# Reordering both ends of the up stage of a hybrid diffusion layer, and loading the gate rows by DMA

## The chip, the cores and the metric

One core of a Trainium2 chip runs the whole kernel. The metric is the device time of one execution in microseconds (us). The kernel before took 1548.68 us, the median of 3 runs (1547.78 to 1554.11).

The core has a matrix engine (TensorE: PE, with its weight loads listed as PEld), three engines that work on rows of 128 partitions (VectorE: DVE; ScalarE: ACT; GpSimd: POOL), and a queue that only issues transfers (SyncE: SP). Each engine takes its own instructions strictly in order; semaphores tie them together. Work is held in SBUF (on-chip memory, 128 partitions) and in eight PSUM banks of 128 x 512 fp32, into which PE accumulates.

## The reference

One layer with 1152 tokens (1024 latent tokens on a 16 x 64 grid, 128 prompt tokens) of width 1024. The part that this change touches is the second half, the convolutional feed-forward network and its gate:

```python
def conv_ffn(h, w_up, conv_w, conv_b, w_down, grid):
    u = dw_conv(h @ w_up, conv_w, conv_b, grid)
    gate, up = jnp.split(u, 2, axis=-1)
    return (jax.nn.silu(gate) * up) @ w_down
...
    x = x + gate1 * mix
    h = rmsnorm(x, norm2) * (1 + scale2) + shift2
    x = x + gate2 * conv_ffn(h, w_ffn_up, ffn_conv, b_ffn_conv, w_ffn_down, grid)
```

`w_up` is 1024 x 5632, `w_down` 2816 x 1024. `dw_conv` is a depthwise convolution: 3 x 3 over the grid for latent tokens, width 3 for prompt tokens. `gate2` is one row of 1024 numbers for the latent tokens and another for the prompt tokens; both come out of a small matrix product early in the kernel. A final `rmsnorm` gives the outputs.

## The kernel before

**Precision.** Each fp32 operand of a large product is split into a high and a low part; a product is three matmuls: high by high, high by low, low by high. The high part is a copy on ACT, the low part a subtraction on DVE or POOL (`split_lo`, L69).

**Up stage (L1742 and around).** The hidden width is cut into 22 columns of 128 gate channels and the 128 up channels that belong to them. For each column the 2 x 2 block product (two halves of the latent tokens, gate and up channels, with the inner dimension of 1024 in two halves) is done with seven products instead of eight, of twelve matmuls of 128 x 512 each. `up(c, p)` issues product p of column c. In the trace they are told apart by the name of their token operand:

- 1: weights 11 by tokens b11, into X; 2: 12 by b21, into Z; 3: s4 by b22, onto Y; 4: 22 by t4, onto X; 5: s1 by t1, into Y; 6: s2 by t2, onto X; 7: s3 by t3, onto X.
- s1 to s4 and t1 to t4 are sums of weight and of token blocks. ACT copies Y after product 5 (`p5`), X after product 1 (`p1`, named cp in the trace) and X after product 6 (`u2`, named u2p). DVE then adds: F (gate channels, two banks) is Z + p1 and Y + u2; S (up channels, two banks) gets its second half as X (after product 7) + p5 (L2081), and X goes on with product 4. So product 4 can't start before that addition has read X, and product 6 and 7 can't start before their copies.
- `up_prompt(c, half)` issues twelve matmuls of 128 x 256 for the prompt tokens (into a bank of the pool x); `prompt_columns(c)` turns them with two transposes (L1987), and ACT and four short DVE instructions convolve them (L1919, L1923).
- The order on PE from column 2 on: 5, then transposes and 4 of the column before, 2, 3, 1, half the prompt, 6, the other half, 7.
- `conv_rows` convolves F and later S: one ACT instruction with the centre weight (L1894), then eight DVE taps (L1906). Then ACT applies silu (L2000), POOL multiplies (L2002) and stores the result to DRAM (`scr_g`, L2003); every second column POOL also makes and stores sums of tokens (`token_sums`, L1859 to L1863).

F and S tiles take turns in three PSUM buffers of two banks (0 and 1, 2 and 3, 4 and 5): S of column c is written where F of column c - 1 was, F of column c + 1 where S of column c - 1 was. The pool x has banks 6 and 7.

**First column.** Column 0 runs beside the end of the stage before it. Its instructions are chained by hand: `run(eng, fn)` puts each one behind the last of its engine. `first_sums` (L1816) makes on DVE the last token sums, the splits of t4 (high parts `half_hi` on ACT, low parts `half_lo` on DVE, in two pieces of 256 tokens), the split of column 1's s1, the weight sums s2 and s4 of column 1, and F's additions; the addition of S follows behind it. Then `second_pair` splits the other weights of column 1 in pairs, copies on ACT and subtractions on POOL.

**Order elsewhere.** Outside those chains a planner orders each engine's instructions when the kernel is built, from program order and from times that it simulates; `tc.issue_after(x)` pins an instruction behind x on its engine. All products of the up stage are chained on PE (`chained`). The order on each engine's queue is then fixed.

**Down stage (L2199).** The down product is again seven products, each over eleven pairs of weight rows and into four PSUM banks (xb or yb), twelve matmuls to a pair. xb are banks 2, 3, 6, 7; yb are banks 0, 1, 4, 5. Weights and activations of a pair come by DMA into one of six raw buffers and are split into one of seven pairs of buffers (`next_w`, `load_w`: load L129, ACT copy L132, subtraction L69 on POOL for the first six pairs, on DVE after that). The planner is free to order the pairs and banks. The first product uses xb, the second yb. `load_gates` at pair 6 of the first product loads a 128 x 512 tile `modrC` with the rows of both gates from DRAM; `make_gates` at pair 10 has PE spread each gate row over 128 partitions, by four fp32 products of a column of the identity with that tile (L2130), into the yb banks; ACT copies them to SBUF (L2131). `add_gated` uses them when the second product is finished.

## Time and profile before

The profiled execution took 1549.85 us; the span from its first to its last instruction is 1548.1 us.

| what | value |
|---|---|
| median of 3 runs | 1548.68 us |
| profiled execution, its span | 1549.85 us, 1548.1 us |
| PE, DVE, ACT, POOL busy | 1487.8, 1145.5, 783.2, 708.9 us |
| first product of column 0 to first down product | 781.25 to 1290.62 us |
| PE waiting in columns 0 and 1: longest | 5.05 us, until 811.01 |
| PE waiting at the last column's product 4 | 1.57 us, until 1287.74 |
| PE waiting in the first down product | 1.92 us, until 1293.37 |
| gate products on PE | 3.67 us, from 1321.94 |
| PE waiting for the gate copies | 1.63 us, until 1329.97 |
| PE waiting after that | none shown |

How to read the rows that follow. A timeline row has the start in us from the span's start, the length in us, engine, line, operation, output and inputs by the program's names, shapes, count, and in brackets the idle time of that engine ahead of it with what ended it. Consecutive like instructions are merged. Matmuls are pipelined: a row's length overlaps the next one's start, so the step from start to start is what counts. A row of a stretch has its bounds and length, then for each engine the busy time and count of instructions, then the PE clock that was granted (1.00 is full), the share of the DMA engines that were busy, and GB/s. A row of waits has who waited, for whom, the total in us, how many times, and the longest.

### The profile page before, as it was taken

To read this page: it belongs to the slowest core of one execution; us is meant where nothing else is said; L and a number is where in the kernel's file an instruction comes from. 1 tells how busy PE (TensorE), PEld (TensorE's weight loads), DVE (VectorE), ACT (ScalarE), POOL (GpSimd) and SP (SyncE) were. 2 spreads that over 40 slices of the span, in tenths; PEclk is the share of its full clock that TensorE was granted. 3 is DMA by queue.
4 is the path that set the end of the run, shared out by engine and by line. 5 is a ranking of instruction groups with operands and counts; after the bars stand their busy time and mean duration, and the time that the engine had idled before them with its cause. 6 is when DMAs were issued, how large, how long until landed. Compare 5 with 4: busy or idle time off the path is not lost.

```text
span 1548.1 us, 31132 instructions
## 1 busy us (share of the span) xinstructions
PE 1487.8 (96%) x12506; PEld 1255.0 (81%) x12506; DVE 1145.5 (74%) x1731; ACT 783.2 (51%) x1523; POOL 708.9 (46%) x538
## 2 busy tenths in 40 slices
PE   7999999999999989899989999999999999999997
PEld 2699998999898978777767888888888887788886
DVE  3657466664556757655789999999999999579575
ACT  3566567555454544512664444444444444467444
POOL 1412122334233240222227999999999996000001
PEclk9999999999999999999999999999999999999999
DMA  9311121335435362677652555545644666879752
GB/s 339 113 54 47 35 65 51 120 92 189 135 123 182 111 198 80 235 272 278 200 180 77 179 166 128 136 118 146 193 117 135 179 162 200 330 244 360 245 192 115
DMA packets 172940, 252.49 MB, mean 163 GB/s; under 512 B 11733, under 2 KB 113603, under 8 KB 170875
## 3 DMA queue, kind: packets, MB, share of 16 engines
q1 hardware_dynamic: 149591, 172.21, 34.8%
q0 software_dynamic: 22592, 77.60, 16.2%
q8 instruction: 98, 1.61, 0.4%
q10 hardware_dynamic: 611, 0.68, 0.1%
q14 instruction: 48, 0.39, 0.1%
HBM read 190.62 MB, written 82.90 MB: 177 GB/s over the span
## 4 chain that ended last, share of the span: by engine, by line
PE 78%; DMA 6%; DVE 6%; issue 4%; ACT 3%; POOL 2%; SPq 1%; POOLq 0%; ACTq 0%; DVEq 0%
PE u L1742 26%; PE mm L603 13%; PE xb L2199 6%; PE yb L2199 6%; PE mm L617 5%; PE x L1970 4%; PE mm L746 3%; PE lv L935 3%; PE yb L2250 2%; PE u L1512 2%; DVE acc L1906 2%; PE x L1003 1%; PE mm L506 1%; DMA mh<-scr_m 1%; DMA wa<-in_w_ada_dram 1%
## 5 line engine op out<-in xcount | busy, mean ns | idle before, releaser
L1906 DVE SCALAR_TENSOR_TENSOR acc<-u,convc,acc 128x945 f32<-128x945 f32 (+2 forms) x352 | 426.8, 1218 | 7.8 <-ACT acc L1894 0.7
L69 POOL TENSOR_TENSOR wl<-raw,wh 128x1024 fp32r<-128x1024 f32 x42 | 103.6, 2468 | 241.0 <-ACT wh L132 183.2
L603 PE MATMUL mm<-h1h,wh 128*128 128x384 f32 x528 | 186.0, 352 | 0.8 <-ACT qj L515 0.8
L603 PE MATMUL mm<-h1l,wh 128*128 128x384 f32 x528 | 180.0, 341 | 0.0
L603 PE MATMUL mm<-h1h,wl 128*128 128x384 f32 x528 | 180.0, 341 | 0.0
L898 DVE TENSOR_TENSOR Q<-Q,fb 128x384 f32<-128x384 f32 x126 | 86.3, 685 | 90.5 <-PE lv L935 89.0
L69 POOL TENSOR_TENSOR wul<-sr,wuh 128x512 fp32r<-128x512 f32 (+1 forms) x64 | 116.2, 1816 | 19.5 <-ACT wuh L1727 19.3
L69 POOL TENSOR_TENSOR wul<-ra,wuh 128x1024 fp32r<-128x1024 f32 x44 | 112.3, 2552 | 20.3 <-ACT wuh L1727 17.8
L888 ACT ACTIVATE m<-k 128x384 f32<-128x384 f32 x126 | 70.2, 557 | 86.9 <-PE lv L935 39.8
L2174 POOL TENSOR_TENSOR sq<-sq,mhalf 128x1 f32<-128x1 f32 x9 | 11.1, 1231 | 213.3 <-DVE sq L2171 213.3
L603 PEld LDWEIGHTS mm<-h1h,wh 128*128 128x128 f32 x528 | 100.3, 190 | 5.7 <-issue 3.9
L603 PEld LDWEIGHTS mm<-h1l,wh 128*128 128x128 f32 x528 | 100.3, 190 | 0.6 <-issue 0.2
L603 PEld LDWEIGHTS mm<-h1h,wl 128*128 128x128 f32 x528 | 100.0, 189 | 0.8 <-issue 0.5
L617 PE MATMUL mm<-wh,h1h 128*128 128x256 f32 x288 | 83.9, 291 | 0.8 <-ACT v L642 0.8
L900 DVE TENSOR_TENSOR k<-k,fb 128x384 f32<-128x384 f32 x126 | 74.2, 589 | 12.2 <-ACT m L888 6.7
L617 PE MATMUL mm<-wh,h1l 128*128 128x256 f32 x288 | 80.5, 280 | 0.0
L617 PE MATMUL mm<-wl,h1h 128*128 128x256 f32 x288 | 80.4, 279 | 0.0
L132 ACT ACTIVATE wh<-raw 128x1024 fp32r<-128x1024 f32 x50 | 53.0, 1059 | 44.0 <-PE mm L603 11.3
L2002 POOL TENSOR_TENSOR acc<-acc,acc 128x1152 f32<-128x1152 f32 x22 | 60.0, 2729 | 9.8 <-DVE acc L1906 9.8
L1727 ACT ACTIVATE wuh<-ra 128x1024 fp32r<-128x1024 f32 x42 | 44.3, 1055 | 39.5 <-issue 16.6
L1934 ACT ACTIVATE u2p<-u 128x512 f32<-128x512 f32 x44 | 26.4, 601 | 70.1 <-PE u L1742 70.1
L1727 ACT ACTIVATE wuh<-sr 128x512 fp32r<-128x512 f32 (+1 forms) x62 | 48.1, 775 | 24.1 <-PE x L1970 16.1
(387 smaller groups left out, 4485.5 us busy)
## 6 DMA issues: line engine op xcount, KB each, us to landing
ra<-in_w_ffn_up_dram SPq DMA_DIRECT2D x84, 256.0 KB, 3.0
raw<-in_w_in_dram SPq DMA_DIRECT2D x32, 512.0 KB, 4.7
v<-in_w_ada_dram SPq DMA_DIRECT2D x27, 512.0 KB, 4.3
scr_g<-acc POOLq DMA_DIRECT2D x22, 576.0 KB, 5.4
scr_s<-late POOLq DMA_DIRECT2D x11, 1024.0 KB, 5.9
scr_t<-in_w_ffn_down_dram POOLq DMA_DIRECT2D x16, 704.0 KB, 7.2
wa<-in_w_ada_dram SPq DMA_DIRECT2D x16, 512.0 KB, 6.2
scr_t<-in_w_ffn_down_dram POOLq DMA_DIRECT2D x2, 2816.0 KB, 13.5
```

Source lines behind the costliest of these rows:

```text
L69: return eng.tensor_tensor(out, full, hi.bitcast(F32), op=ALU.subtract)
L603: anchor["fill"] = mm(ps, a[:, kt, :], h[kt][b], start=(n == 0), stop=(n == 23))
L617: anchor["fill"] = mm(ps, h[kt][t // 3][:, ts_], a[:, kt % 4, :], start=(n == 0), stop=(n == 23))
L888: nc.scalar.activation(aps(t, 0, [[2 * h, NB], [h, 2], [1, h]]), aps(src, 0, [[2 * h, NB], [BL + h, 2], [1, h]]), AF.Copy)
L898: nc.vector.tensor_tensor(qm, qm, aps(ff_, 2 * h - 1, [[BL - h, 2], [2 * h, NB], [0, h]]), op=ALU.mult)
L900: nc.vector.tensor_tensor(km, km, aps(ff_, BL + 2 * h - 1, [[-(BL + h), 2], [2 * h, NB], [0, h]]), op=ALU.mult)
L1727: first = nc.scalar.activation(hi, raw, AF.Copy)
L1742: last = mm(dst, w_slot(c, a, x)[:, kt, :], HB[y][b][:, kt, :], start=(start and n == 0), stop=(stop and n == 11), skip_group_check=True,)
L1906: last = nc.vector.scalar_tensor_tensor(o, u3[:, r0 + dy : r1 + dy, c0 + dx : c1 + dx], wc(3 * (dy + 1) + dx + 1), o, op0=ALU.mult, op1=AL ...
L1970: last = mm(pk, HB[h]["p"][:, 4 * half + kt, :], aps(flat(W[x]), a * 512 + kt * P, [[(b - a) * 512, 2], [1, P]]), start=(half + kt + n == ...
L2002: last = nc.gpsimd.tensor_tensor(accg, accg, accu, op=ALU.mult)
L2199: anchor["down"] = mm(banks[i], w[a][:, ts_], w[b][:, 512:1024], start=(start and j == 0 and n == 0), stop=(j == NPAIR - 1 and n == 2), sk ...
```

## The change

Four edits, none of which changes what is computed:

1. **First column.** The addition of S and the first addition of F move from the end of DVE's chain to a place right behind the last token sums, ahead of the t4 splits. The low parts of t4 move ahead of the weight sums s2 and s4. The issue of product 7 moves ahead of `first_sums` in the text.
2. **Last column.** Column 21's products go in the order 2, 1, 3, 6, half the prompt, 7, the other half, 4 and then the prompt's transposes, instead of 2, 3, 1, half the prompt, 6, the other half, 7, transposes, 4.
3. **First down banks.** The first three pairs of the first down product are done bank by bank, nine matmuls to a bank, in the order of the banks (2, 3, 6, 7), pinned behind the last product of the up stage.
4. **Gate rows.** The tile `modrC`, the four spreading products and their copies are gone; four DMAs on SP's queue each load a half row of a gate from DRAM into all 128 partitions, at pair 6 of the first down product.

```diff
--- before.py
+++ after.py
@@ -1815,10 +1815,12 @@
 
     def first_sums():
 
-        F = u[0][0]
+        F, S = u[0]
         for n in range(2):
             token_sum(tmp[2 + n], rb(1, 0, n), tmp[2 + n])
         new_tiles("t4", 1)
+        run("dve", lambda: tt(S[:, 512:NS], S[:, 0:512], copies["p5"], op=ALU.add))
+        run("dve", lambda: tt(F[:, 0:512], F[:, 0:512], copies["p1"], op=ALU.add))
         half_hi("t4", 0, tmp[2])
         slot = SLOT[1]["s1"]
         hi, lo = (flat(W[x][:, slot]) for x in "hl")
@@ -1826,11 +1828,10 @@
         run("act", lambda: nc.scalar.activation(hi, raw, AF.Copy))
         run("dve", lambda: split_lo(nc.vector, lo, raw, hi))
         half_hi("t4", 1, tmp[3])
+        for n in range(2):
+            half_lo("t4", n, tmp[2 + n])
         run("dve", lambda: second_sum("s2", "s1", "11", ALU.subtract, nc.vector))
         run("dve", lambda: second_sum("s4", "12", "s2", ALU.subtract, nc.vector))
-        for n in range(2):
-            half_lo("t4", n, tmp[2 + n])
-        run("dve", lambda: tt(F[:, 0:512], F[:, 0:512], copies["p1"], op=ALU.add))
         run("dve", lambda: tt(F[:, 512:NS], F[:, 512:NS], copies["u2"], op=ALU.add))
 
     token_work()
@@ -2022,7 +2023,11 @@
             up(c, 5)
         if c == 0:
             prompt_work()
-        if c > 0:
+        if c == NHID:
+            up(c - 1, 4)
+            prompt_columns(c - 1)
+            second_half(c - 1)
+        elif c > 0:
             prompt_columns(c - 1)
             up(c - 1, 4)
             second_half(c - 1)
@@ -2032,9 +2037,11 @@
             split_slots(n, ("21", "22"), nc.gpsimd)
             if n + 1 < NHID:
                 load_row(n + 1, 2)
+        last_c = c == NHID - 1
         if c > 0:
             up(c, 2)
-            up(c, 3)
+            if not last_c:
+                up(c, 3)
         pks[c] = ps_p.tile([P, 2 * P], F32, name="x", tag="x")
         if c == 1:
             up_prompt(c, 0)
@@ -2042,9 +2049,14 @@
         if c > 0:
             u[c].append(ps_u.tile([P, NS], F32, name="u", tag="u"))
             up(c, 1)
-        if c > 1:
+            if last_c:
+                up(c, 3)
+        if 1 < c and not last_c:
             up_prompt(c, 0)
         up(c, 6)
+        if last_c:
+            up_prompt(c, 0)
+            up(c, 7)
         if c == 0:
             up(c, 3)
             up_prompt(c, 0)
@@ -2055,8 +2067,8 @@
                 load_row(n + 1, 1)
         F, S = u[c]
         if c == 0:
+            up(c, 7)
             first_sums()
-            up(c, 7)
         else:
             nc.vector.tensor_tensor(F[:, 0:512], F[:, 0:512], copies["p1"], op=ALU.add)
             nc.vector.tensor_tensor(F[:, 512:NS], F[:, 512:NS], copies["u2"], op=ALU.add)
@@ -2077,9 +2089,9 @@
         if c > 0 and n:
             split_slots(n, ("s2", "s4"), nc.gpsimd)
         if c > 0:
-            up(c, 7)
-        add_s = lambda: nc.vector.tensor_tensor(S[:, 512:NS], S[:, 0:512], copies["p5"], op=ALU.add)
-        run("dve", add_s) if c == 0 else add_s()
+            if not last_c:
+                up(c, 7)
+            nc.vector.tensor_tensor(S[:, 512:NS], S[:, 0:512], copies["p5"], op=ALU.add)
         anchor["conv"] = conv_rows(F, c, acc[c][0])
         if c == 0:
             ran["act"] = anchor["rows"]
@@ -2113,22 +2125,13 @@
     smp = pool(ctx, "sm2", 1)
     fn = gpp.tile([P, D], F32, name="fn")
     gate2 = {}
-    modr["C"] = gpp.tile([P, 512], F32, name="modrC")
-
     def load_gates():
-        with tc.issue_after(anchor["load"].ins):
-            nc.sync.dma_start(modr["C"], scr_mod["C"])
-
-    def make_gates():
-
         for v in (1, 0):
             gate2[v] = gpp.tile([P, D], F32, name=f"gate2_{v}")
             for half in range(2):
-                pt = ps_c[half].tile([P, 512], F32, name="yb", tag="yb")
                 rr = 32 * (2 + half) + v
-                with tc.issue_after(anchor["down"].ins):
-                    mm(pt, ident[:, rr : rr + 1].to_broadcast([P, P]), modr["C"], start=True, stop=True)
-                nc.scalar.activation(gate2[v][:, HF[half]], pt, AF.Copy)
+                with tc.issue_after(anchor["load"].ins):
+                    nc.sync.dma_start(gate2[v][:, HF[half]], scr_mod["C"][rr : rr + 1, :].to_broadcast([P, 512]))
 
     g_ph = gpp.tile([P, NHID, P], F32R, name="g_ph")
     g_pl = gpp.tile([P, NHID, P], F32R, name="g_pl")
@@ -2185,9 +2188,9 @@
         with tc.issue_after(anchor["load"].ins):
             nc.sync.dma_start(fn, ins["final_norm"].rearrange("(o d) -> o d", o=1).to_broadcast([P, D]))
 
-    def product(banks, start, stop, done, tail=0, beside={}):
-
-        for js in [(j,) for j in range(NPAIR - tail)] + ([tuple(range(NPAIR - tail, NPAIR))] if tail else []):
+    def product(banks, start, stop, done, tail=0, head=0, beside={}):
+
+        for js in ([tuple(range(head))] if head else []) + [(j,) for j in range(head, NPAIR - tail)] + ([tuple(range(NPAIR - tail, NPAIR))] if tail else []):
             ws = [next_w() for _ in js] if len(js) == 1 else next_ws(len(js))
 
             if js[0] in beside:
@@ -2196,14 +2199,15 @@
                 ts_ = slice(i * P, (i + 1) * P)
                 for j, w in zip(js, ws):
                     for n, (a, b) in enumerate(((0, 0), (0, 1), (1, 0))):
-                        anchor["down"] = mm(
-                            banks[i],
-                            w[a][:, ts_],
-                            w[b][:, 512:1024],
-                            start=(start and j == 0 and n == 0),
-                            stop=(j == NPAIR - 1 and n == 2),
-                            skip_group_check=True,
-                        )
+                        with tc.issue_after(anchor["down"].ins) if j < head else nullcontext():
+                            anchor["down"] = mm(
+                                banks[i],
+                                w[a][:, ts_],
+                                w[b][:, 512:1024],
+                                start=(start and j == 0 and n == 0),
+                                stop=(j == NPAIR - 1 and n == 2),
+                                skip_group_check=True,
+                            )
                 if js[-1] == NPAIR - 1:
                     done(i)
 
@@ -2218,8 +2222,9 @@
         return [p.tile([P, 512], F32, name=nm, tag=nm) for p in pool_ for _ in range(2)]
 
     xb = bank(ps_b, "xb")
+    anchor["down"] = ran["pe"]
     p1, u2, u3 = {}, {}, {}
-    product(xb, True, False, copy_bank(p1, "p1"), beside={6: load_gates, 10: make_gates})
+    product(xb, True, False, copy_bank(p1, "p1"), beside={6: load_gates}, head=3)
 
     yb = bank(ps_c, "yb")
 
```

## The prediction

> **What bounds the kernel now.** I read the busy shares first, then stretches of the up stage, then who waits for whom, then the timelines of TensorE (PE), VectorE (DVE), ScalarE (ACT) and GpSimd (POOL) at both ends of the up stage.
>
> ```profile
> PE 1487.8 (96%) x12506; PEld 1255.0 (81%) x12506; DVE 1145.5 (74%) x1731; ACT 783.2 (51%) x1523; POOL 708.9 (46%) x538
> ```
>
> ```profile
> 811.00:816.30 5.30, 5.29 (x13) 4.13 (x14) 4.78 (x7) 2.12 (x4) 4.56 (x4) 0.50 0.19 53
> ...
> 850.00:895.00 45.00, 45.00 (x223) 37.29 (x222) 43.74 (x47) 20.93 (x28) 42.53 (x29) 1.00 0.60 190
> ```
>
> ```profile
> 1294.00:1299.00 5.00, 5.00 (x17) 3.94 (x16) 4.89 (x5) 0.78 (x1) 4.46 (x4) 0.66 1.07 259
> ```
>
> ```profile
> DVE u L2061 <- ACT cp L1934: 1.0, 6, 0.2
> ```
>
> ```profile
> PEld u L1742 <- DVE acc L1906: 6.2, 20, 0.3
> ```
>
> In a stretch row stand the busy times of PE, its weight loads, DVE, ACT and POOL, then the granted PE clock. PE is the bound overall, but in the middle of the up stage (two columns in 45 us) DVE is busy for 43.74 of 45.00 us too. The two hold each other once per column: product 1 (b11) writes the bank that the convolution of the column before has just read (20 waits of 0.3 us on DVE acc L1906), and DVE's first addition waits for the copy of that product (up to 0.2 us). So a gain of PE alone at the front of the up stage is kept only as far as DVE moves too. Two stretches run at half or lowered clock (0.50 and 0.66); each follows an idle PE.
>
> **First column.**
>
> ```profile
> 801.21 0.28 PE L1970 MATMUL x<-wuh,ph 128*128 128x256 f32 x1
> ...
> 805.58 0.38 PE L1987 MATMUL x<-ident,late 128*128 128x128 f32 x2
> 811.01 0.79 PE L1742 MATMUL u<-t4h,wuh 128*128 128x512 f32 x1 [5.05 <-DVE u L2081]
> ...
> 816.29 0.45 PE L1742 MATMUL u<-b21h,wuh 128*128 128x512 f32 x1
> ```
>
> ```profile
> 798.44 2.35 DVE L1377 TENSOR_TENSOR acc<-rb,acc 128x1024 f32<-128x1024 f32 x2
> ...
> 804.38 4.51 DVE L69 TENSOR_TENSOR t4l<-acc,t4h 128x1024 fp32r<-128x1024 f32 x2
> ...
> 810.27 0.68 DVE L2081 TENSOR_TENSOR u<-u,u2p 128x512 f32<-128x512 f32 x1
> ...
> 811.69 1.20 DVE L1906 SCALAR_TENSOR_TENSOR acc<-u,convc,acc 128x945 f32<-128x945 f32 x1 [0.49 <-ACT acc L1894]
> ...
> 814.45 12.43 DVE L1906 SCALAR_TENSOR_TENSOR acc<-u,convc,acc 128x945 f32<-128x945 f32 x10
> 828.57 0.70 DVE L2061 TENSOR_TENSOR u<-u,cp 128x512 f32<-128x512 f32 x1 [1.70 <-ACT cp L1934]
> ```
>
> ```profile
> 804.50 1.06 ACT L1727 ACTIVATE wuh<-sr 128x1024 fp32r<-128x1024 f32 x1
> ...
> 810.45 1.21 ACT L1894 ACTIVATE acc<-u,vcol,convc 128x1024 f32<-128x1024 f32 x1 [3.60 <-DVE u L1834]
> ```
>
> ```profile
> 804.65 3.15 POOL L69 TENSOR_TENSOR wul<-ra,wuh 128x1024 fp32r<-128x1024 f32 x1 [17.79 <-ACT wuh L1727]
> ```
>
> PE is ready for product 4 at 805.7 and waits until the addition of S (L2081) has read the bank, at 811.0; then its twelve matmuls take 5.28 us (811.01 to 816.29) at clock 0.50, where twelve take 2.72 at full clock (1268.82 to 1271.54, quoted below). In the changed order that addition stands behind the token sums: product 7 ends at 801.2, so it runs 801.4 to 802.1, F's first half to 802.7, the s1 split to 803.3. The first t4 split then takes about 1.2 (a sum of that size, L1377, is half of 2.35); the second falls into POOL's split and takes what it took there, 4.51 / 2 = 2.25: done at 806.6. The place of product 7 in the text changes nothing on PE, whose order here is a written chain. Product 4 starts at once with its first matmul, waits 0.8 for the split, and ends near 809.1: PE gains 7.2 us here.
>
> What is late next: the sums s2 and s4 now follow the t4 splits and end near 808.3. Behind them, F's second addition ends at 808.9. On ACT's queue the copy of the s2/s4 pair (804.50 before) goes at 808.4, the 21/22 copy behind it to 810.4, and the convolution's first ACT step (1.21 us, L1894) stands behind both. So DVE's first tap starts at 811.6, as in the trace. POOL's splits of s2/s4 come about 4 us later, but product 3 needs them only from 811.9: no stall over 0.2. Eight taps of 1.24 (12.43 / 10) bring F's convolution to 821.3. Product 1 of column 1 writes that bank. PE is there at 817.6 (809.1, two products of 2.73, the wait of 0.2, 24 prompt steps of 0.117, as in the last column below): **the stall moves there, 3.7 us**, probably with some slow clock. DVE then has four taps of S to do and reaches the addition L2061 at 826.3 rather than 828.57: its idle 1.70 is gone and so are the short prompt taps that stood between. I take **-2.3 us**. Bounds: -1.3 if the stall lowers the clock through all of product 1 (12 x 0.2 = 2.4 us later, 1 us of it seen by DVE), and -7.2 if DVE follows PE all the way.
>
> **Last column.**
>
> ```profile
> 1268.82 0.39 PE L1742 MATMUL u<-b21h,wuh 128*128 128x512 f32 x1
> ...
> 1271.54 0.39 PE L1742 MATMUL u<-b22h,wuh 128*128 128x512 f32 x1
> ...
> 1274.34 0.50 PE L1742 MATMUL u<-b11h,wuh 128*128 128x512 f32 x1
> ...
> 1277.19 0.28 PE L1970 MATMUL x<-wuh,ph 128*128 128x256 f32 x1
> ...
> 1278.60 0.40 PE L1742 MATMUL u<-t2h,wuh 128*128 128x512 f32 x1
> ...
> 1285.79 0.38 PE L1987 MATMUL x<-ident,late 128*128 128x128 f32 x2
> 1287.74 0.50 PE L1742 MATMUL u<-t4h,wuh 128*128 128x512 f32 x1 [1.57 <-DVE u L2081]
> ...
> 1290.62 0.39 PE L2199 MATMUL xb<-wuh 128*128 128x512 f32 x1
> ...
> 1293.37 0.47 PE L2199 MATMUL xb<-wuh 128*128 128x512 f32 x1 [1.92 <-DVE acc L1923]
> ...
> 1294.14 0.51 PE L2199 MATMUL xb<-wuh 128*128 128x512 f32 x1
> ...
> 1297.78 0.39 PE L2199 MATMUL xb<-wuh 128*128 128x512 f32 x1
> ```
>
> ```profile
> 1273.09 4.79 DVE L1906 SCALAR_TENSOR_TENSOR acc<-u,convc,acc 128x945 f32<-128x945 f32 x4
> 1278.02 0.70 DVE L2061 TENSOR_TENSOR u<-u,cp 128x512 f32<-128x512 f32 x1
> ```
>
> Product 1 moves ahead of product 3. But it waits for the convolution of column 20, whose last tap is the first of the four at 1273.09 and ends at 1274.3; PE would be there at 1271.54. So PE idles 2.8 us. From 1274.34 on: product 1 2.85, product 3 2.73, product 2 2.75 (with the loss after a copy), half the prompt 1.41 (1277.19 to 1278.60), product 7 2.75, the other half 1.41, product 4 2.72, the two transposes 0.13: the first bank of the down product starts at 1291.1, **+0.5 us** against 1290.62. Product 4's wait of 1.57 is gone, since half the prompt covers the addition; the copies ahead of products 2 and 7 are covered by product 3 and the prompt. The prompt columns' two ACT steps and four short taps come some 5 us later on their queues, the same in number; only the down banks, next, wait for them. The new idle may lower the clock: I add **+1.0** (seven in ten of 1.5, the loss in the stretch from 1294: 3.64 us for ten steps that take 2.27 at full clock), bounds 0 and +1.7.
>
> [...]
>
> **First down banks.** Now the planner has PE begin with the banks of the prompt tiles, and one of them is still read by the prompt taps (1.92 us); after that the clock falls. From 1290.62 to 1297.78 sixteen matmul steps take 7.16 us instead of 16 x 0.227 = 3.63. The written order begins with the banks of column 20's S, whose taps stand ahead of column 21's sixteen; the last twelve of those begin at 1293.14 (quoted below), so those banks are free by 1288. They take 18 matmuls (4.1 us), then come nine on one prompt bank (2.0 us): the bank that was late is wanted 6.2 us after the transposes. Before, it came free 1293.37 - 1285.9 = 7.4 us after them, 2 of these because ACT had splits ahead. I count the whole **-3.5**, bound 0.
>
> **Gate rows.**
>
> ```profile
> 1320.90 0.39 PE L2199 MATMUL xb<-wuh 128*128 128x512 f32 x1
> 1321.94 3.67 PE L2130 MATMUL yb<-modrC,ident 128*128 128x512 f32 x8 [0.20 <-DMA modrC<-scr_modC]
> 1325.05 0.79 PE L2199 MATMUL xb<-wuh 128*128 128x512 f32 x1
> ...
> 1329.97 0.50 PE L2199 MATMUL yb<-wh 128*128 128x512 f32 x1 [1.63 <-ACT gate L2131]
> ```
>
> ```profile
> 1293.14 14.92 DVE L1906 SCALAR_TENSOR_TENSOR acc<-u,convc,acc 128x1008 f32<-128x1008 f32 x12
> ...
> 1309.11 5.94 DVE L69 TENSOR_TENSOR wul<-sr,wuh 128x1024 fp32r<-128x1024 f32 x2
> ```
>
> ```profile
> SPq L2120 <- DMA scr_g<-acc: 5.8, 1, 5.8
> ```
>
> ```profile
> 1318.46 0.32 SPq L2120 DMA_DIRECT2D modrC<-scr_modC  x1
> ```
>
> The gate matmuls hold PE from 1321.6 (1320.90 and three steps) to 1325.05, 3.5 us, and 0.2 in the next matmul; their four ACT copies hold the second product's banks for 1.63. All that goes: **-5.3**. In its place four loads of 256 KB go through SP's queue, three more than now, 0.32 us each; the queue stood waiting there (5.8 us for one store alone), the gates are wanted only when the second product ends some 30 us later, and the memory they fill was the t1 tokens', used for the last time ahead of 1268. The old load waited until 1318.46 for a store out of the last accumulators' memory and held the weight loads behind it; that goes as well. I take the loads at nothing; if they did push a weight load, one pair's time (12 x 0.227 = 2.7 us) is the bound.
>
> With PE 8.7 us earlier, DVE's weight splits are next: taps end at 1308.0, then one split per pair, the third done at 1315.05; PE wants that one at 1291.1 + 108 x 0.227 = 1315.6. It just holds, and bounds any further gain here.
>
> **Sum.** -2.3 + 0.5 + 1.0 - 3.5 - 5.3 = -9.6. The profiled execution took 1549.85 (span 1548.1), 1.2 above the median of the runs, 1548.68. 1549.85 - 9.6 = 1540.2 for a like execution, **1539.0 us** as the median.
>
> **Rivals.**
> 1. The new stalls eat the down banks' gain: the late prompt bank is still late (a wait of 2 us or more at the fourth bank), the clock falls again, so -3.5 shrinks to 0 and +1.0 becomes +1.7: 1539.0 + 4.2 = 1543.2. For it: only 0.5 us of margin at that bank and an order that can't pass it; against: ACT has fewer splits ahead.
> 2. DVE follows PE in the first column and the whole 7.2 is kept: 1539.0 - 4.9 = 1534.1. For it: the planner may put the convolution's first ACT step ahead of the copies; against: the DVE taps are a fixed amount of work.
> [...]
> 4. Slower: the planner orders all columns anew from shifted times, and puts the addition L2061 one tap earlier in each. Between product 1's start (1274.34) and that addition lie 3.68 us, which three taps fill now; with two, DVE idles 1.2 us per column, 20 columns: +24, 1563. It decides from 0.5 us per column. For it: column 1 and the later ones already differ (four and three taps); against: nothing inside those columns is edited.
>
> **How the numbers follow.** Forecast 0.55 (own range 1536.5 to 1541.5), rival 1 0.20, rival 2 0.12, rival 3 0.06, rival 4 0.07. The range takes in rivals 1 and 2: 1533.9 to 1545.0. A measurement of this kernel can tell 0.5%, 7.7 us, from no change. Faster than 1540.9: most of the forecast (0.50) and rivals 2 and 3, 0.68. Slower: rival 4, 0.07. Within: 0.25.
>
> **What would show it.** No wait of 5 us on L2081 and no clock of 0.50 near 811; instead a wait of 3 to 4 us of product 1 on DVE acc in column 1, and L2061 at 826 to 827. A wait of 2.5 to 3 us ahead of product 1 in the last column. No wait at product 4 there nor at the first down banks. No gate matmuls, and the second down product some 9 us earlier against the last column's product 6. Wrong would be: L2061 unmoved, a period per column other than the present 22.5 (45 for two), or PE waiting for a weight split between 1308 and 1320.

## The result, and the profile after

The changed kernel took 1542.0 us (median of 5 runs, 1540.39 to 1542.78), the kernel before 1550.27 in the runs beside it (5 runs, 1547.78 to 1554.11): a ratio of 0.9947, 95% interval 0.9934 to 0.9961. A second measurement gave 0.9961 (0.9947 to 0.9974). It is faster, by about half a percent, on the line between "faster" and "within" as the prediction drew it. The forecast of 1539.0 is 3 us too low; the range holds the time. About half of the 3 us is the comparison: the kernel before was 1.6 us slower in these runs than the 1548.68 that the forecast starts from. As a ratio the forecast is 0.9937, inside the first interval and outside the second.

The profiled execution took 1542.0 us (span 1540.2). Line numbers of the changed kernel are shifted: its additions stand at L1822 (S, column 0), L2073, L2074 (F) and L2094 (S), the taps at L1907 and L1924, the first ACT steps at L1895, the copies at L1935, the down products at L2203, the gate loads at L2134.

One execution starts its up stage earlier or later than another (775.5 to 783.7 us in the fourteen traces of this study, ahead of every edited instruction), so stages are compared from milestone to milestone: the first product of the up stage, the last column's first product (b21h, first matmul), the first matmul of the down stage (xb), the first of its second product (yb). From the PE timelines, in us:

| stage | before | after | difference | forecast |
|---|---|---|---|---|
| up to the first product | 781.25 | 779.90 | -1.35 | 0 |
| first product to last column | 487.57 | 487.15 | -0.42 | -2.3 |
| last column | 21.80 | 23.70 | +1.90 | +1.5 |
| first down product | 39.35 | 31.46 | -7.89 | -8.8 |
| rest of the span | 218.13 | 217.99 | -0.14 | 0 |

The edited stages give -6.4 where -9.6 was forecast. The other two stages, which no edit touches, give -1.5 more in this pair of executions; that part is luck. First the five longest waits of PE from the up stage to the second down product, in the changed kernel (columns: who, for whom, total, times, longest):

```profile
PE u L1742 <- DVE acc L1907: 7.2, 2, 4.6
PE u L1742 <- ACT u2p L1935: 1.7, 2, 1.5
PE u L1742 <- ACT cp L1935: 1.0, 1, 1.0
PE xb L2203 <- POOL wul L69: 0.9, 1, 0.9
PE u L1742 <- POOL wul L69: 0.7, 1, 0.7
```

The waits that the prediction took away are gone: 5.05 on the addition of S, 1.57 at product 4 of the last column, 1.92 on a prompt bank, the gate copies. Those it announced are there: product 1 of column 1 (4.6 where it said 3.7) and product 1 of the last column (2.64 in brackets; counted from start to start, as the forecast's 2.8 was, it is 5.52 - 2.72 = 2.80). Two waits on POOL's `wul` it did not expect: 0.90 in the first down product, and 0.66 ahead of product 3 of column 1, where it said no stall over 0.2; that one costs nothing here, since product 1 waits right behind it. Next the first column, PE's rows with a wait and then DVE:

```profile
811.39 0.50 PE L1742 MATMUL u<-b22h,wul 128*128 128x512 f32 x1 [0.66 <-POOL wul L69]
821.37 0.56 PE L1742 MATMUL u<-b11h,wuh 128*128 128x512 f32 x1 [4.56 <-DVE acc L1907]
826.99 0.50 PE L1742 MATMUL u<-t2h,wuh 128*128 128x512 f32 x1 [1.03 <-ACT cp L1935]
831.48 0.50 PE L1742 MATMUL u<-t3h,wuh 128*128 128x512 f32 x1 [1.47 <-ACT u2p L1935]
```

```profile
800.08 0.70 DVE L1822 TENSOR_TENSOR u<-u,u2p 128x512 f32<-128x512 f32 x1 [0.63 <-PE u L1742]
...
801.88 2.35 DVE L69 TENSOR_TENSOR t4l<-acc,t4h 128x1024 fp32r<-128x1024 f32 x2
804.15 2.89 DVE L1802 TENSOR_TENSOR sr<-sr,ra 128x512 f32<-128x512 f32 x1
...
807.69 0.69 DVE L1835 TENSOR_TENSOR u<-u,u2p 128x512 f32<-128x512 f32 x1
...
810.94 1.20 DVE L1907 SCALAR_TENSOR_TENSOR acc<-u,convc,acc 128x945 f32<-128x945 f32 x1 [1.93 <-ACT acc L1895]
...
813.70 13.73 DVE L1907 SCALAR_TENSOR_TENSOR acc<-u,convc,acc 128x945 f32<-128x945 f32 x11
827.35 0.69 DVE L2073 TENSOR_TENSOR u<-u,cp 128x512 f32<-128x512 f32 x1
...
849.15 0.70 DVE L2073 TENSOR_TENSOR u<-u,cp 128x512 f32<-128x512 f32 x1
```

The additions come early as planned (800.08), product 4 no longer waits. But the first tap of F's convolution starts at 810.94, 31.0 us after the up stage's first product; before, it was 811.69, 30.4 after. Its input was ready at 808.4; it waits for ACT's first step. On ACT, in the changed kernel:

```profile
807.80 1.06 ACT L1727 ACTIVATE wuh<-sr 128x1024 fp32r<-128x1024 f32 x1 [2.18 <-DVE sr L1802]
808.77 1.04 ACT L1727 ACTIVATE wuh<-ra 128x1024 fp32r<-128x1024 f32 x1
809.72 1.19 ACT L1895 ACTIVATE acc<-u,vcol,convc 128x1024 f32<-128x1024 f32 x1
```

That is the queue the prediction described. So the convolution's end, and with it product 1 of column 1, comes no earlier than that order lets it, and the stall of 4.56 brings lowered clock with it. Stretches of the changed kernel (bounds, length, busy times of PE, PEld, DVE, ACT, POOL, then granted clock):

```profile
818.00:824.00 6.00, 2.63 (x7) 2.09 (x8) 5.86 (x6) 4.72 (x5) 5.36 (x4) 0.80 0.05 14
824.00:830.00 6.00, 4.97 (x19) 3.41 (x17) 5.89 (x6) 1.23 (x3) 5.92 (x5) 0.91 0.49 143
850.00:895.00 45.00, 45.00 (x222) 37.28 (x221) 43.74 (x47) 20.99 (x29) 43.53 (x29) 1.00 0.61 199
1272.00:1277.00 5.00, 4.43 (x13) 3.59 (x14) 4.89 (x5) 1.17 (x1) 2.73 (x3) 0.66 0.90 346
1294.00:1299.00 5.00, 5.00 (x24) 4.08 (x23) 5.00 (x7) 1.27 (x2) 5.00 (x3) 1.00 1.03 399
```

In the 45 us of two columns DVE is busy for the same 43.74, and from the addition of column 2 to that of column 3 it is 22.54 us in both kernels: the period is unchanged. The slow clock has left the first down banks (0.66 before, 1.00 now) and turned up behind the last column's new wait (0.66 from 1272). The last column and the first down product on PE:

```profile
1267.05 0.39 PE L1742 MATMUL u<-b21h,wuh 128*128 128x512 f32 x1
...
1272.57 0.79 PE L1742 MATMUL u<-b11h,wuh 128*128 128x512 f32 x1 [2.64 <-DVE acc L1907]
...
1290.75 0.48 PE L2203 MATMUL xb<-wuh 128*128 128x512 f32 x1
...
1293.50 0.50 PE L2203 MATMUL xb<-wul,wuh 128*128 128x512 f32 x1 [0.90 <-POOL wul L69]
...
1322.21 0.39 PE L2203 MATMUL yb<-wh 128*128 128x512 f32 x1
```

No wait on a prompt bank and no gate products. The wait of 0.90 has its cause on POOL: it ends with the second split of the down weights. First the kernel before, then the changed one:

```profile
1282.46 2.42 POOL L69 TENSOR_TENSOR wul<-sr,wuh 128x1024 fp32r<-128x1024 f32 x1
```

```profile
1290.66 2.79 POOL L69 TENSOR_TENSOR wul<-sr,wuh 128x1024 fp32r<-128x1024 f32 x1
```

The planner's new order puts the down weights' first splits later: ACT's copies for them go behind the copy of product 6 (from 1282.98 instead of 1278.80, 4 us), and POOL's subtractions behind the gated product and its stores (8 us). The four gate loads go through SP's queue at once, and no row shows a wait caused by them:

```profile
1301.38 1.84 SPq L2134 DMA_DIRECT2D gate<-scr_modC  x4
```

### The profile page after: what moved, and what is told of

It reads as the page before. It is cut to its first block, busy times and chain, and to the rows that moved or that the text cites. A ratio compares the mean times of both kernels' runs of the same rounds, so it can differ in the third digit from the quotient of the medians.

```text
span 1540.2 us, 31113 instructions
## 1 busy us (share of the span) xinstructions
PE 1480.9 (96%) x12498; PEld 1252.3 (81%) x12498; DVE 1146.1 (74%) x1731; ACT 781.3 (51%) x1519; POOL 707.4 (46%) x538
## 4 chain that ended last, share of the span: by engine, by line
PE 78%; DMA 6%; DVE 6%; issue 4%; ACT 3%; POOL 2%; SPq 1%; POOLq 0%; ACTq 0%; DVEq 0%
PE u L1742 25%; PE mm L603 13%; PE xb L2203 8%; PE yb L2203 6%; PE mm L617 5%; PE x L1971 3%; PE mm L746 3%; PE lv L935 3%; PE yb L2255 2%; PE u L1512 2%; PE x L1003 1%; PE mm L506 1%; DVE acc L1907 1%; DMA mh<-scr_m 1%; DMA wa<-in_w_ada_dram 1%
## 5 line engine op out<-in xcount | busy, mean ns | idle before, releaser
L1907 DVE SCALAR_TENSOR_TENSOR acc<-u,convc,acc 128x945 f32<-128x945 f32 (+2 forms) x352 | 426.8, 1218 | 10.3 <-ACT acc L1895 3.2
L69 POOL TENSOR_TENSOR wl<-raw,wh 128x1024 fp32r<-128x1024 f32 x42 | 103.0, 2464 | 241.1 <-ACT wh L132 184.4
L898 DVE TENSOR_TENSOR Q<-Q,fb 128x384 f32<-128x384 f32 x126 | 81.4, 646 | 91.5 <-PE lv L935 90.0
L69 POOL TENSOR_TENSOR wul<-sr,wuh 128x512 fp32r<-128x512 f32 (+1 forms) x64 | 115.7, 1808 | 20.1 <-ACT wuh L1727 20.0
L69 POOL TENSOR_TENSOR wul<-ra,wuh 128x1024 fp32r<-128x1024 f32 x44 | 112.8, 2564 | 17.9 <-ACT wuh L1727 17.8
L1935 ACT ACTIVATE u2p<-u 128x512 f32<-128x512 f32 x44 | 26.5, 601 | 76.4 <-PE u L1742 74.9
```

Of the source, the lines that this page charges most:

```text
L69: return eng.tensor_tensor(out, full, hi.bitcast(F32), op=ALU.subtract)
L898: nc.vector.tensor_tensor(qm, qm, aps(ff_, 2 * h - 1, [[BL - h, 2], [2 * h, NB], [0, h]]), op=ALU.mult)
L1907: last = nc.vector.scalar_tensor_tensor(o, u3[:, r0 + dy : r1 + dy, c0 + dx : c1 + dx], wc(3 * (dy + 1) + dx + 1), o, op0=ALU.mult, op1=AL ...
```

## The experiments

Ratios are to the kernel before, run beside each kernel on the same chip. Beside the ratio, the trace of each kernel gives the stages from milestone to milestone: the span from the up stage's first product to DVE's addition of column 2, to the last column, then the last column and the first down product.

| kernel | ratio (95%) | to addition, column 2 | to last column | last column | first down product |
|---|---|---|---|---|---|
| before | 1 | 69.50 | 487.57 | 21.80 | 39.35 |
| after (edits 1 to 4) | 0.9947 (0.9934 to 0.9961) | 69.25 | 487.15 | 23.70 | 31.46 |
| e1: edit 1 | 0.9980 (0.9970 to 0.9990) | 69.68 | 487.55 | 21.78 | 38.04 |
| e2: edit 2 | 1.0016 (1.0005 to 1.0027) | 68.60 | 486.63 | 23.44 | 41.48 |
| e3: edit 3 | 1.0010 (0.9998 to 1.0023) | 68.31 | 486.42 | 21.78 | 40.84 |
| e4: edit 4 | 0.9959 (0.9944 to 0.9975) | 69.80 | 487.79 | 21.78 | 33.74 |
| e5: after, again | 0.9961 (0.9947 to 0.9974) | 69.83 | 487.82 | 23.87 | 31.33 |
| e6: edits 1, 3, 4 | 0.9937 (0.9915 to 0.9958) | 69.21 | 487.20 | 21.79 | 30.33 |
| e7: after, F's second addition early | 0.9959 (0.9942 to 0.9976) | 70.22 | 488.10 | 23.44 | 31.71 |
| e8: e7 without edit 2 | 0.9926 (0.9909 to 0.9944) | 69.21 | 487.68 | 21.81 | 30.29 |
| e9: e8, copy first on ACT | 0.9934 (0.9920 to 0.9948) | 67.98 | 486.00 | 21.79 | 30.31 |
| e10: after, three taps less | 0.9961 (0.9948 to 0.9975) | 69.08 | 487.10 | 23.83 | 31.48 |
| e11: after, wait filled | 0.9987 (0.9976 to 0.9998) | 69.28 | 487.20 | 22.28 | 35.92 |
| e12: edits 3, 4 | 0.9932 (0.9916 to 0.9947) | 69.25 | 487.17 | 21.80 | 30.34 |

**e1: the first column's edit alone.**

```diff
         new_tiles("t4", 1)
+        run("dve", lambda: tt(S[:, 512:NS], S[:, 0:512], copies["p5"], op=ALU.add))
+        run("dve", lambda: tt(F[:, 0:512], F[:, 0:512], copies["p1"], op=ALU.add))
...
+        for n in range(2):
+            half_lo("t4", n, tmp[2 + n])
         run("dve", lambda: second_sum("s2", "s1", "11", ALU.subtract, nc.vector))
         run("dve", lambda: second_sum("s4", "12", "s2", ALU.subtract, nc.vector))
-        for n in range(2):
-            half_lo("t4", n, tmp[2 + n])
-        run("dve", lambda: tt(F[:, 0:512], F[:, 0:512], copies["p1"], op=ALU.add))
...
```

> The first edit alone: both accumulator additions of the first column directly behind the sums they read, ahead of the token splits; last column, down banks and gate rows as before. The prediction's step: 2.3 us below the kernel before. The theory from the two traces (the additions come 8 us earlier on VectorE, but the first tap waits for ScalarE's part of the sum, which stands behind ScalarE's pair copies and these behind the splits, so that the first tap starts no earlier and VectorE idles 1.3 us on the second addition's part later): 0 to 1.0 us below, taken at 0.4. If TensorE's whole stall of the first column were won: 7.2 us below.

The timed ratio is 3.1 us of gain, but the stage that the edit is in gained nothing: 487.55 against 487.57. The trace shows 1.3 in the first down product, where one pair of weight loads now stands ahead of the load of `modrC` on SP's queue and the gate copies come 1.3 us earlier, counted from the first down matmul. The rest of the 3.1 is not in any stage of the profiled execution, which was the slowest of e1's twelve (1548.44 against a median of 1545.74). e6 and e12 below, with and without edit 1 beside edits 3 and 4, show none of it.

**e2: the last column's order alone.**

```diff
             up(c, 2)
-            up(c, 3)
+            if not last_c:
+                up(c, 3)
...
             up(c, 1)
+            if last_c:
+                up(c, 3)
```

> The last column's product order alone. The prediction's step: 1.5 us slower than before (0.5 of new stall balance, 1.0 of slow clock). The theory from the two traces: 1.9 us slower in the last column, as the changed kernel's trace has it (21.80 to 23.70), if nothing behind takes it back. A rival: here the gate products by TensorE still stand behind the first down product and wait for the modulation row, which VectorE's last convolution sets, so what the last column loses is taken back there and the time is within 0.5 us of before; the first down banks' stall of 5 us could also shrink by as much as TensorE comes later, with the same answer.

Slower by 0.16%, and not made up behind. PE in the last column and in the first down product, then the stretch of the wait:

```profile
1274.28 0.50 PE L1742 MATMUL u<-b11h,wuh 128*128 128x512 f32 x1 [2.64 <-DVE acc L1906]
...
1289.20 0.50 PE L1742 MATMUL u<-t4h,wuh 128*128 128x512 f32 x1 [0.89 <-DVE u L2092]
...
1298.63 0.77 PE L2210 MATMUL xb<-wuh 128*128 128x512 f32 x1 [5.49 <-DVE acc L1923]
```

```profile
1272.00:1277.00 5.00, 2.72 (x12) 2.27 (x13) 4.93 (x6) 1.17 (x1) 4.02 (x4) 1.00 0.97 307
```

The wait ahead of product 1 is the same 2.64 as in the changed kernel, but here the clock stays at 1.00: from product 1 to product 3 it takes 2.85 us instead of 4.26. PE then comes to product 4 sooner than the addition of S (L2092) is done, and waits 0.89 for it. The last column is 23.44, so the full clock is worth only 0.26 against the changed kernel's 23.70. e7 has the same 2.64, 2.85, 0.89 and 23.44.

With the transposes behind product 4 the prompt taps come later, and the first down product, still in the planner's order of banks, waits 5.49 for them instead of 1.92. The rival that the loss would be taken back falls. Together with edit 2 the bank order of edit 3 is needed.

**e3: the first down banks alone.**

```diff
-    product(xb, True, False, copy_bank(p1, "p1"), beside={6: load_gates, 10: make_gates})
+    anchor["down"] = ran["pe"]
+    product(xb, True, False, copy_bank(p1, "p1"), beside={6: load_gates, 10: make_gates}, head=3)
...
-        for js in [(j,) for j in range(NPAIR - tail)] + ...
+        for js in ([tuple(range(head))] if head else []) + [(j,) for j in range(head, NPAIR - tail)] + ...
```

> The third edit alone: the first down product takes banks that are free early, the gate rows are still made by TensorE behind it. The prediction's step, counted as a term of its own: 3.5 us faster than before. The theory of the chain: about no change (within 0.7), because the gate products wait for the modulation row that comes from the last convolution, and TensorE would only reach that wait 3.5 us earlier; the gain exists only with the fourth edit.

No gain: 1.0010. The stages have 1.5 more in the first down product, and 2.6 more in the rest of the span (220.74 against 218.13). PE there:

```profile
1317.66 3.67 PE L2130 MATMUL yb<-modrC,ident 128*128 128x512 f32 x8 [3.05 <-DMA modrC<-scr_modC]
...
1327.66 0.79 PE L2200 MATMUL yb<-wh 128*128 128x512 f32 x1 [3.59 <-ACT gate L2131]
```

The banks are free and the clock is full in the first down matmuls (1.00 from 1290 to 1310), as edit 3 meant; PE reaches the gate products early and waits 3.05 for the row that they spread and 3.59 (1.63 before) for their copies. Behind the second wait its matmuls start 0.43 us apart until 1333.4, where 0.23 is the step at full clock; the granted clock from 1320 to 1330 is 0.83, where it was 1.00 in the kernel before. The chain theory holds in kind, the additive one falls: alone, the saving of edit 3 turns into a longer wait for what edit 4 removes.

**e4: the gate loads alone.**

```diff
-                pt = ps_c[half].tile([P, 512], F32, name="yb", tag="yb")
...
-                with tc.issue_after(anchor["down"].ins):
-                    mm(pt, ident[:, rr : rr + 1].to_broadcast([P, P]), modr["C"], start=True, stop=True)
-                nc.scalar.activation(gate2[v][:, HF[half]], pt, AF.Copy)
+                with tc.issue_after(anchor["load"].ins):
+                    nc.sync.dma_start(gate2[v][:, HF[half]], scr_mod["C"][rr : rr + 1, :].to_broadcast([P, 512]))
```

> The fourth edit alone: gate rows by broadcast loads, the first down product still with the banks it had. The prediction's step, as a term of its own: 5.3 us faster than before (gate products and copies gone). The theory of the two traces: from the first down product's start to the second's the whole change has 7.9 us less, so 7.9 less what the banks give (3.5 by the prediction): 4.4 to 5.3 faster. If broadcast loads collided with the weights' loads it would be under 3.

6.3 us faster by the ratio (7.2 by the medians), 5.61 less in the first down product. The prediction said 5.3. The wait on the prompt bank stands as before:

```profile
1291.10 0.47 PE L2190 MATMUL xb<-wuh 128*128 128x512 f32 x1 [1.93 <-DVE acc L1923]
```

**e5 to e8: with and without the last column's order, F's second addition early or not.** e5 is the changed kernel again. e6 is the changed kernel with the last column as before (the lines of e2 taken back). e7 is the changed kernel with one line moved, and e8 has both.

```diff
         run("dve", lambda: tt(F[:, 0:512], F[:, 0:512], copies["p1"], op=ALU.add))
+        run("dve", lambda: tt(F[:, 512:NS], F[:, 512:NS], copies["u2"], op=ALU.add))
...
         run("dve", lambda: second_sum("s4", "12", "s2", ALU.subtract, nc.vector))
-        run("dve", lambda: tt(F[:, 512:NS], F[:, 512:NS], copies["u2"], op=ALU.add))
```

> The changed kernel once more, on the chip and against the runs of the next three: 0.9934 to 0.9961 of the kernel before, as it measured (1539 to 1544 us here). It is the row that the next three are compared with. If the four edits only added up (3.6 less, 2.2 more, 0.7 more, 7.2 less by the medians of the single edits) it would be 7.9 below the kernel before; the traces say that the orders of the last column and of the down banks each lose alone and need each other and the gate loads.

> The change without its second edit: last column's products in the order of before, the other three edits kept. The traces' theory: the wait of 2.64 ahead of product 1 is gone (23.70 to 21.78 in the last column), and the wait of 0.90 on GpSimd's split too, since ScalarE's splits come early again; product 4's wait of 1.57 returns and is contained in the 21.78. VectorE's weight splits bound the rest: 1.0 to 2.5 us faster than the changed kernel. Rival (the order of the last column is what frees the down banks): a wait on the prompt banks returns at the fourth bank, with slow clock, and the time is 1 to 3 us slower than the changed kernel.

> The changed kernel with F's second addition moved directly behind F's first one, ahead of the splits of product 4's token and of the sums s2 and s4, so that ScalarE's first step of F's convolution no longer stands behind its pair copies. The theory of the traces (the first column gained 0.4 instead of 2.3 because this step held the convolution at its old start): the first tap starts at about 806 instead of 810.9, product 1 of column 1 waits under 2 us instead of 4.56, the addition L2073 comes about 3 us earlier, and the time is 2 to 4 us below the changed kernel; part of it may be lost where product 4 waits up to 2 us for its later token split. Rival (VectorE's work in the first column is a fixed amount and sets the column's end): within 0.7 us of the changed kernel.

> Both: F's second addition early and the last column's order of before. If both theories hold and add up, 3 to 6.5 us below the changed kernel, 1536 to 1539 us; if the weight splits of VectorE bound the last column, the two share the gain and it is 2 to 3.5 below.

e5 came out at 0.9961, the upper edge of what was expected. e6 is 0.9937 against it (2.1 us less by the medians); the two intervals overlap, but the stages say where it comes from: 2.1 less in the last column (21.79 against 23.87) and 1.0 less in the first down product, whose wait on POOL is gone, since the splits are early again. The rival, a wait on the prompt banks, does not appear: the bank order of edit 3 is enough by itself.

e7 moved PE but not the time. Its rows on PE and on ACT:

```profile
818.54 0.50 PE L1742 MATMUL u<-b11h,wuh 128*128 128x512 f32 x1 [0.37 <-DVE acc L1907]
825.44 0.80 PE L1742 MATMUL u<-t2h,wuh 128*128 128x512 f32 x1 [3.88 <-ACT cp L1935]
```

```profile
822.27 1.16 ACT L2001 ACTIVATE acc<-acc 128x1152 f32<-128x1152 f32 x1
823.34 1.04 ACT L1727 ACTIVATE wuh<-ra 128x1024 fp32r<-128x1024 f32 x1
824.29 0.61 ACT L1727 ACTIVATE wuh<-sr 128x512 fp32r<-128x512 f32 x1
824.81 0.57 ACT L1935 ACTIVATE cp<-u 128x512 f32<-128x512 f32 x1
```

The stall of 4.56 on the convolution is down to 0.37: product 1 comes 2.4 us earlier (39.03 after the first product instead of 41.47). But its copy now stands on ACT behind the silu of column 0 and two split copies, so product 6 waits 3.88 for it instead of 1.03, 2.85 more. Of the 2.4 us, 1.2 are left at product 6, and these go into the clock: behind that wait the matmuls of product 6 start 0.43 us apart, where 0.23 is the step at full clock (by the ratio of the steps, an estimate, a clock of 0.53), and product 6 takes 6.17 until product 7 instead of 4.49. Product 7 comes 52.10 after the up stage's first product, in the changed kernel 51.58. The 2 to 4 us that were expected did not arrive.

e8 is 0.9926, 3.9 us less than e5 by the medians, inside the 3 to 6.5 that were expected, but not for the reason given. Its stages are those of e6 (487.68, 21.81 and 30.29 against 487.20, 21.79 and 30.33): what it has over e5 is the last column's old order, and no stage shows a gain of the early addition. Its first column has the same products as e7's, and yet product 6 takes 5.30 in it, 0.87 less, and column 2's addition comes 1.0 earlier: behind the wait (3.76, in e7 3.88) its steps are 0.43 us over 3.4 us and 0.23 after that, in e7 0.43 to the end of the product. So much did the clock behind one wait differ.

**e9: the copy ahead of the splits.** To e8, in column 1:

```diff
-            copy(c, "p1", X)
+            anchor["p1"] = copy(c, "p1", X)
...
-            split_slots(n, ("s1",), nc.gpsimd)
-            split_slots(n, ("11", "12"), nc.gpsimd)
+            with tc.issue_after(anchor["p1"].ins) if c == 1 else nullcontext():
+                [split_slots(n, x, nc.gpsimd) for x in (("s1",), ("11", "12"))]
```

> F's second addition early and the last column's order of before, and besides, in column 1, ScalarE's split copies of the next weights (s1 and the 11/12 pair) are put behind the copy of product 1, so that this copy stands directly behind the Silu of column 0. The theory that ScalarE's queue ate the gain of the early addition: the copy goes 1.4 us earlier (22.1 to 20.7 us after product 7's bank was free, by the trace without this edit), TensorE's wait of 3.8 for it falls to about 2.4, VectorE's addition of column 1 comes 1.5 us earlier and column 2's 1 to 1.5 earlier (67.7 to 68.2 us after the up stage's first product, against 69.21); the time falls by 1 to 1.5. Rival (VectorE's work up to column 2 is a fixed amount and already without gaps that count): column 2's addition at 69.2 again, the time within 0.5 us of the kernel without this edit.

Column 2's addition comes at 67.98 after the first product instead of 69.21, the 1 to 1.5 us that were expected of ACT's queue. From product 6 on, PE in e9 is PE in e8 shifted by as much: product 6 at 44.53 instead of 45.79, product 7 at 49.82 instead of 51.09. The last column starts 1.7 earlier; where the other 0.45 comes from is not shown. PE:

```profile
822.93 0.57 PE L1742 MATMUL u<-t2h,wuh 128*128 128x512 f32 x1 [2.45 <-ACT cp L1935]
```

The wait for the copy fell from 3.8 to 2.45. This is one trace, and the same first column differs by 1.0 between e7 and e8; in the timed runs the gain is below what can be told apart (0.9934 against 0.9926, on different chips).

**e10: three taps less on VectorE.** In the changed kernel; the output lacks the contribution of the next grid row in column 0's up channels:

```diff
-                if dy == 0 and dx == 0:
+                if (dy == 0 and dx == 0) or (ch == 22 and dy == 1):
                     continue
```

> The changed kernel, with three of the eight VectorE taps of column 0's second convolution left out (those of the next grid row), so the output is not the reference's. They touch no bank that product 1 of column 1 waits for. Theory that VectorE's amount of work sets where column 2 begins, whatever TensorE does: column 2's addition comes 3.7 us earlier (three taps of 1.24), 65.5 us after the up stage's first product instead of 69.25, and the last column starts 3.7 earlier too. Rival, the chain through TensorE and ScalarE sets it: 69.25 as before, VectorE idles 3.7 us more. In between, both hold each other and it comes 1 to 2 us earlier.

69.08 instead of 69.25 to 69.83: nothing of the 3.7 us arrived. DVE only waits longer:

```profile
830.20 0.69 DVE L2073 TENSOR_TENSOR u<-u,cp 128x512 f32<-128x512 f32 x1
834.32 0.70 DVE L2074 TENSOR_TENSOR u<-u,u2p 128x512 f32<-128x512 f32 x1 [3.43 <-ACT u2p L1935]
...
851.87 0.70 DVE L2073 TENSOR_TENSOR u<-u,cp 128x512 f32<-128x512 f32 x1 [0.95 <-ACT cp L1935]
```

The three taps stood behind column 1's addition: five taps of S are still ahead of it, and it comes at 47.41 as in the changed kernel (47.45). From there on VectorE's amount of work is not what sets column 2's start. The chain does: end of F's convolution, product 1, its copy on ACT, product 6, its copy, product 7.

**e11: the last column's wait filled.** In the changed kernel:

```diff
-            up(c, 2)
+            [up(c, 2) for _ in range(2 if last_c else 1)]
```

> The changed kernel with product 2 of the last column computed twice (twelve matmuls, about 2.7 us, the same values into the same bank), so that TensorE works through the 2.64 us in which it waited ahead of product 1. If the idle time lowered the clock, as the prediction counted with 1.0 us: product 1 then runs at full clock, and from the last column's first product to the down product it takes 22.6 to 23.0 us instead of 23.70. [...] The whole time moves by no more than 1 us either way.

```profile
1269.01 0.39 PE L1742 MATMUL u<-b21h,wuh 128*128 128x512 f32 x1
...
1274.54 0.50 PE L1742 MATMUL u<-b11h,wuh 128*128 128x512 f32 x1
...
1291.29 0.48 PE L2203 MATMUL xb<-wuh 128*128 128x512 f32 x1
...
1295.01 0.50 PE L2203 MATMUL xb<-wul,wuh 128*128 128x512 f32 x1 [1.86 <-POOL wul L69]
...
1303.92 0.50 PE L2203 MATMUL xb<-wul,wuh 128*128 128x512 f32 x1 [1.81 <-POOL wul L69]
```

```profile
1272.00:1277.00 5.00, 5.00 (x23) 3.88 (x22) 4.93 (x6) 1.17 (x1) 4.18 (x3) 1.00 0.95 286
```

Product 1 starts at the same place (5.53 after the last column's first matmul, 5.52 without the filler), so the added work cost nothing, and what follows takes 16.75 instead of 18.18. The clock is 1.00 instead of 0.66, and from product 1 to product 3 it takes 2.85 instead of 4.26. That alone would not have shortened the column, as e2 and e7 show, where product 4 then waits. In e11 it does not wait: DVE's weight split (L69) ahead of the addition of S takes 1.22 instead of 2.77, and the addition starts 18.18 after the column's first matmul and not 19.71. In the changed kernel:

```profile
1286.76 0.69 DVE L2094 TENSOR_TENSOR u<-u,u2p 128x512 f32<-128x512 f32 x1
```

The whole last column takes 22.28, under the 22.6 to 23.0 that were expected; the 1.42 are the slow clock and product 4's wait together. But the kernel as a whole got slower than the changed one, against the expectation of 1 us at most: POOL's order came out different, two of its splits now hold PE for 1.86 and 1.81, and the first down product takes 35.92.

**e12: banks and gate loads alone.** The kernel before with the diffs of e3 and e4.

> The third and fourth edits alone: down banks and gate loads, both ends' product orders and VectorE's additions as before. The theory of the traces (the first edit is worth nothing once column 1 has waited for F's convolution, the second costs 1.9 to 3): from the up stage's first product to the last column 486.4 to 487.8 as in the other traces without the first edit, the last column 21.8, the first down product 30.3, and the time is that of the kernel with edits one, three and four: 0.9937 of the kernel before, within 0.0015. Rival (the first edit is worth the 3.1 us that its run alone showed in the timed medians): 0.9937 + 0.0020 = 0.9957.

0.9932, the same as with edit 1 (e6, 0.9937) and within 0.0006 of the lowest ratio here (e8); the rival at 0.9957 lies outside the interval. The stages are those of e6 to a twentieth of a microsecond. Edits 3 and 4 alone are 0.53 to 0.84% faster than the kernel before and carry all of the gain; PE's only wait left from the last column to the second down product is the old one at product 4:

```profile
PE u L1742 <- DVE u L2081: 1.6, 1, 1.6
```

## Why the prediction was right or wrong

**First column, -2.3: wrong, no gain is seen.** Five traces with the edit in its given form (after, e1, e5, e6, e11) have 487.15 to 487.82 from the first product to the last column, mean 487.38; five without it (before, e2, e3, e4, e12) have 486.42 to 487.79, mean 487.12. The -0.42 of the first comparison is inside that spread. The steps up to the stall were right: additions at 800 instead of 810, product 4 without a wait, first tap where it was, product 1 of column 1 as the next to wait.

The step that failed is "DVE then has four taps of S to do and reaches the addition L2061 at 826.3 rather than 828.57". That is 45.05 after the first product. Measured are 47.45, and 47.32 before: the addition is unmoved, which the prediction itself had named as a sign of being wrong. The 2.4 us add up from the rows: the first tap was 0.7 later than forecast, two short prompt taps still stood between the long ones (0.5), and the planner put five taps of S ahead of the addition, not four (1.2). The eleven taps from 813.70 are the last six of F and five of S; the ten from 814.45 in the kernel before were six and four. DVE does not wait ahead of the addition, but four taps would have gained no more than 0.4: the copy that it reads ends on ACT at 826.94.

On PE, product 1 starts at 41.47, where the forecast had 40.05 and the kernel before 43.39. From product 1 to product 6 it then takes 5.62 us instead of 3.95, at a clock of 0.80 and 0.91 where it was 1.00, so that product 6 comes only 0.25 earlier (47.09 against 47.34). From there the copies of products 1 and 6 set the pace: e10 shows that DVE's taps do not, and in e9 the copy that was moved ahead of two splits passes its 1.2 us on. The prediction's own lower bound of -1.3, "if the stall lowers the clock through all of product 1", had a part of the mechanism and still left too much.

**Last column, +1.5: 0.4 short, and one step held by luck.** The wait came as forecast (2.80 from start to start), and in the changed kernel the clock fell behind it: 1.41 us in product 1 (forecast +1.0, bound +1.7). The order by itself costs 0.48 (22.28 in e11 against 21.80; forecast +0.5). But the step "Product 4's wait of 1.57 is gone, since half the prompt covers the addition" held only because the slow clock brought PE there late: product 4 starts 20.81 after the column's first matmul, the addition ends at 20.40, and at full clock PE would have been there at 19.40. In e2 and e7 the clock stayed full and product 4 waited 0.89. So of the two costs the column pays one or the other, 23.44 with the wait and 23.70 to 23.87 with the slow clock (after, e5, e10). In the prediction's list of steps from 1274.34 on, "product 2" behind product 3 is product 6; the time that it counts is right.

Behind the idle of 2.64 the granted clock in the changed kernel was 0.50 from 1272.57 to 1275.30, with 0.43 us from matmul to matmul; the same steps of 0.43 stand there in e5 and e10. In the other two traces that have this wait (e2, e7) the steps are 0.23. Rival 3, the sum without the +1.0 for the clock, falls for the changed kernel; and its 1538.0 would have needed the addition of S earlier too.

**First down banks and gate rows, -3.5 and -5.3: right, but 0.9 of the 8.8 was given back.** Without the last column's new order (e12) both together are 39.35 - 30.34 = 9.0. Gate loads alone are 5.61, and the banks on top of them 3.40: each term within 0.3 of its forecast. The banks' 3.5 exists only together with the gate loads (e3), a condition that the prediction does not name; with both edits in, its sum holds. In the changed kernel 1.1 of the 9.0 is lost to what the prediction left out: the last column's new order moves the copies of the first down weights 4 us back on ACT and the subtractions 8 us on POOL, and PE waits 0.90 for one of them and restarts. The prediction had checked DVE's weight splits for lateness, not POOL's earlier ones. Rival 1 (a late prompt bank, 1543.2) did not occur, though its time lies nearer to the measured one than the forecast does.

**What went as said besides:** the period of 22.5 is unchanged (rival 4 falls), no row shows a load hurt by the gates' DMAs, PE did not wait for a split by DVE. Rival 2 (the whole 7.2 kept) falls. From the forecast to the result: first column +1.9 to +2.3, last column +0.4, first down product +0.9. That is 3.2 to 3.6 in the edited stages; the times came 1.5 nearer to the forecast in the profiled pair by what varies between executions elsewhere, which is luck.

## What to carry to other kernels

A stall that is removed at the head of a pipelined stage is worth what the whole chain behind it lets through: follow it past the next engine's queue (here ACT's copies behind its splits) before counting a gain, and test an engine suspected as the bound by taking work from it. Edits that meet in one place should be costed together: here the free banks were worth nothing without the gate loads, and the last column's new order, which removes a wait of its own, cost 3 us once the banks no longer needed it. When a planner orders the other engines, an edit of one engine's order moves the others' work too; look for what comes later there, not only for what the edit names, and count the instructions ahead of a milestone again in the new order. A loss of clock that hides a wait is not a loss that can be won back by itself (here the last column took 23.70 us with the slow clock and 23.44 without it): look for the wait behind it.

## What the runs showed of the hardware

Whether TensorE's clock fell behind an idle of 2.64 us differed between executions of the same products. In five traces PE waits 2.64 us ahead of product 1 of the last column. In three of them (after, e10, e5) the matmuls of product 1 then start 0.43 us apart for 2.7 to 3.2 us (granted clock in after 0.50 from 1272.57 to 1275.30), and the product takes 4.26, 4.39 and 4.44 until the next one; in two (e2, e7) they start 0.23 apart (granted clock in e2 1.00 from 1272 to 1277) and product 1 takes 2.85. PE's steps ahead of the idle are the same in all five; what decides is not shown. With one product of filler in place of the wait the granted clock was 1.00 from 1272 to 1277 (e11).

What a stall of 5 us cost in clock differed as well: in five traces in which product 4 of column 0 waits 5.02 to 5.05 us on the unedited first column, its matmuls start 0.43 us apart at first (granted clock in before 0.50 from 811.00 to 816.30), for 2.7 us in e3 and through the whole product in before and e4; it takes 4.18, 4.45, 5.11, 5.28 and 5.28 us (e3, e2, e12, before, e4), and product 1 of column 1 starts 12.45, 12.73, 13.40, 13.63 and 13.90 us after it. What decides how long the slow steps last is not shown. Where the stall ended at another place (after, e1, e5, e6, e11) the same distance was 16.79 to 16.83 each time, because there the end of the convolution sets it (product 1 waits 4.49 to 4.60 for it). The up stage so differed by 1.4 us between kernels with the same first column, about what an edit of this size is worth.

Not settled: why the timed runs of e1 show 3.1 us of gain while the stages of its profiled execution show 1.3, and why the up stage started between 775.5 and 783.7 us.
